# Two-layer hybrid decoder step: the means of squares by a constant 128x128 stationary matrix, the inverse root over 128x264

## The chip, the cores and the metric

The kernel runs on one core of one Trainium2 chip. The metric is device microseconds of one execution; the median of three runs of the kernel before is 2299.41 us (2299.01 to 2299.87). A core has TensorE (PE, matrix products into PSUM), VectorE (DVE), ScalarE (ACT), GpSimd (POOL) and SyncE (SP, here only a queue that issues DMAs). Each engine executes its own queue in program order and waits at semaphores for the others.

## The reference

One inference step over 256 prompt tokens and 8 sample tokens (264 columns), model width 2048, two layers:

```python
def rmsnorm(x, g):
    y = x * lax.rsqrt(jnp.mean(x * x, axis=-1, keepdims=True) + 1e-6)
    return y * g

# one layer
p = rmsnorm(h, norm1_g) @ w_in                  # 2048 -> 10 groups of 512
a, bg, cg, hh, q, k, v, g, u, vv = split(p, 10)
y_a = pool_mixer(a); y_b = conv_mixer(bg, cg, hh)
on  = layernorm_f32(retention(q, k, v))         # over the 128 channels of each of 4 heads
y_c = silu(g) * on * ret_norm_g
y_d = sgu_mixer(u, vv)
h = h + concat(y_a, y_b, y_c, y_d) @ w_out
gt, up = split(rmsnorm(h, norm2_g) @ w_gate_up, 2)
h = h + (silu(gt) * up) @ w_down                # inner width 5632
# after both layers
y = rmsnorm(h, final_norm_g)
```

The mixers' states are outputs too. The change touches the five RMS norms and the two retention layer norms.

## The kernel before, in words

Activations lie transposed: channels on the 128 partitions, the 264 tokens on the free axis, so `h` is 16 tiles of 128x264. Every weight matrix is read once, in sub-blocks of 8 blocks of 128x128 (512 KB each) by SP's queue into seven `raw` buffers. Each sub-block is split into a high part (`whi`, a ScalarE cast, L270) and a remainder (`wlo`, a VectorE subtraction, L271 through the helper of L120); there are four buffers of each, and `do_split` is called at the start of each sub-block so that three further ones are ready or on their way. The activations are split in the same way, and each 128x128x264 block takes three matmuls in a fast f32 form (`work`, L283): low weight by high activation, high by low, high by high. An output chunk (128 channels) of an inner width of 2048 is two sub-blocks, 48 matmuls. Results collect in four PSUM buffers `acc`; four others, `misc`, serve everything else.

`run` (L300) goes over the chunks of a phase: `work`, then `evac` (the chunk is read out of PSUM by VectorE), then `step()`, which advances each background task (a Python generator) by one `yield`. This fixes the queue of every engine: within VectorE's, a chunk's two weight splits, its evacuation, the background work of its step, then the next chunk's splits. The phases of a layer are "in" (40 chunks, in the order V/K/Q x4, VV, U, G, A, then CG/HH/BG x4), "out" (16 chunks), and three times gate/up and down.

The RMS norm is applied late. The phase before adds the squares of `h` (Square on ScalarE, sums on POOL) into partial sums 128x264; the weights are multiplied with the unnormalised activations, and the evacuation multiplies by the token's inverse root `r`. `rms.stats()` is called after 12 of the first chunk's 16 blocks and `rms.bcast()` later in the second chunk (in the first input phase, which works on four chunks at once, behind the second and the third of them). `stats` calls `token_rsqrt` (L157): the partial sums are the stationary operand, 88 tokens at a time, a column of 1/2048 is the moving one, so the sums arrive with tokens on partitions, 88x3 for the RMS norm. VectorE then takes the inverse root of this small tile in eleven operations (`rsqrt`, L137: a shift, a subtraction from a constant, three Newton steps). `token_bcast` (L172) brings it back to 128 partitions of 264 columns with three matmuls against the identity, and ScalarE copies it to SBUF (L205).

The retention norm is the background task `ret_norm` (L545): per step and head a centring product (L551) with its square and copy on ScalarE; then one `token_rsqrt` for all four heads (88x12); then, head by head in four steps, the broadcast, two VectorE multiplies, and a split of the result into the high and low operand of the "out" phase. Other tasks in the same chunks: `sgu` (L571), `pool` (L452), the convolution in the evacuations of HH and BG.

At the end (L733 to L739) the last norm's `r` is used directly from PSUM by VectorE and from SBUF by POOL to scale the 16 tiles of `h`, which nine DMAs write out.

Of the kernel before, what the change touches and what calls it, by code (L numbers as in the profile page):

```python
# [13 lines left out]
AF = mybir.ActivationFunctionType  # L14
ALU = mybir.AluOpType
AX = mybir.AxisListType

P = 128
L = 2
D = 2048  # L20
KD = D // P
NP = 256
NS = 8
T = NP + NS
# [5 lines left out]
EPS = 1e-6  # L30
# [8 lines left out]
TB = 88  # L39
# [12 lines left out]
def hybrid_step(ctx, tc, I, O):  # L52
    nc = tc.nc
    pe, ve, se, po, sy = nc.tensor, nc.vector, nc.scalar, nc.gpsimd, nc.sync
# [4 lines left out]
    def mk(name, shape, dt=F32):  # L59
        return sb.tile(shape, dt, tag=name, name=name)  # L60

    H4 = [mk(f"h{i}", [P, 4, T]) for i in range(4)]
    h = [H4[k // 4][:, k % 4, :] for k in range(KD)]
# [14 lines left out]
    ident, cent = (sq128[:, i, :] for i in range(2))  # L78
    ccol = mk("ccol", [P, 6 + 4 * 16 + KD])
    kdec, rcnt = ccol[:, 0:4], ccol[:, 6:70].rearrange("p (g t) -> p g t", g=4)  # L80
    mean128, mean2048, gfin = ccol[:, 4:5], ccol[:, 5:6], ccol[:, 70:70 + KD]
# [17 lines left out]
    vns = mk("vns", [NS, GW])  # L99
    i8w = mk("i8w", [NS, 4, NS])  # L100
    stat = mk("stat", [P, 12])
    small = mk("small", [P, 3, 12])

    def ta():
        return tfree.popleft()

    def tf(*ts):
        tfree.extend(ts)

    def ma():  # L110
        return misc.popleft()

    def mf(*ts):
        misc.extend(ts)

    def mm(out, lhsT, rhs, start=True, stop=True):
        pe.matmul(out, lhsT, rhs, start=start, stop=stop)  # L117

    def tt(out, a, b, op, eng=None):
        (eng or ve).tensor_tensor(out=out, in0=a, in1=b, op=op)  # L120

    def stt(out, a, s, b, op0, op1):
        ve.scalar_tensor_tensor(out=out, in0=a, scalar=s, in1=b, op0=op0, op1=op1)  # L123

    def ts(out, a, s1, s2, op0, op1, eng=None):
        if s2 is None:
            (eng or ve).tensor_scalar(out=out, in0=a, scalar1=s1, scalar2=None, op0=op0)
        else:
            (eng or ve).tensor_scalar(out=out, in0=a, scalar1=s1, scalar2=s2, op0=op0, op1=op1)
# [4 lines left out]
    def f(ap):  # L134
        return ap.bitcast(F32)

    def rsqrt(out, m, t):  # L137
        ts(t.bitcast(I32), m.bitcast(I32), 1, None, ALU.logical_shift_right, None)
        ts(out.bitcast(I32), t.bitcast(I32), -1.0, float(0x5F3759DF), ALU.mult, ALU.add)
        for _ in range(3):  # L140
            stt(t, out, -0.5, out, ALU.mult, ALU.mult)
            tt(t, t, m, ALU.mult)
            stt(out, t, 1.5, out, ALU.add, ALU.mult)

    def split(src):
        hi, lo = rfree.popleft(), rfree.popleft()
        se.copy(hi[:], src)  # L147
        tt(lo[:], src, f(hi[:]), ALU.subtract)
        return hi, lo
# [4 lines left out]
        stt(lo[:], src, s, f(hi[:]), ALU.mult, ALU.subtract)  # L154
        return hi, lo

    def token_rsqrt(srcs, wcol):  # L157
        n = len(srcs)
        ps = ma()
        for c in range(3):  # L160
            cc = slice(c * TB, (c + 1) * TB)
            for i, parts in enumerate(srcs):
                for x, part in enumerate(parts):
                    mm(ps[:TB, c * n + i:c * n + i + 1], part[:, cc], wcol, x == 0, x == len(parts) - 1)
        w = 3 * n
        m, t, r = (small[:TB, q, :w] for q in range(3))
        ts(m, ps[:TB, :w], EPS, None, ALU.add, None)
        mf(ps)
        rsqrt(r, m, t)
        return r  # L170

    def token_bcast(ps, r, i, n):  # L172
        for c in range(3):
            mm(ps[:, c * TB:(c + 1) * TB], r[:, c * n + i:c * n + i + 1].to_broadcast([TB, P]), ident[:TB, :TB])

    class Rms:
        def __init__(self, second=KD - 1):
            self.parts = []
            self.second = second
            self.n = 0  # L180

        def add(self, src, eng=None):
            s = ta()
            if eng:
                tt(s[:, :T], src, src, ALU.mult, eng)
            else:
                se.activation(s[:, :T], src, AF.Square)  # L187
            if self.n in (0, self.second):
                self.parts.append(s)
            else:  # L190
                a = self.parts[-1]
                tt(a[:, :T], a[:, :T], s[:, :T], ALU.add, po if self.n < self.second else ve)
                tf(s)
            self.n += 1

        def stats(self):
            assert self.n == KD
            self.r = token_rsqrt([[p[:, :T] for p in self.parts]], mean2048)
            tf(*self.parts)

        def bcast(self, both=False):
            ps = ma()
            token_bcast(ps, self.r, 0, 1)
            r = ta()
            se.copy(r[:, :T], ps[:, :T])  # L205
            mf(ps)
            return (r, ps) if both else r

    def to_x(k, gcol):
        scaled(XH[k][:], h[k], gcol)  # L210
        stt(XL[k][:], h[k], gcol, f(XH[k][:]), ALU.mult, ALU.subtract)
# [149 lines left out]
    def in_phase(l, cs, rms, hooks=None):  # L361
        X = {}

        def bcast():
            r = X["r"] = rms.bcast()
            X["rt"] = []
            rt = X["rt"] = [ta() for _ in range(4)]
            for i in (2, 3, 0, 1):
                tt(rt[i][:, :T], tabs[:, i, :], r[:, :T], ALU.mult, po)
            if l == 0:  # L370
                layer_loads(0)
# [179 lines left out]
        def ret_norm():  # L551
            sq, xc = {}, {}
            yield
            for j in range(4):
                yield
                ps = ma()
                mm(ps[:, :T], cent, oT[j][:, :T])
                sq[j], xc[j] = ta(), ta()
                se.activation(sq[j][:, :T], ps[:, :T], AF.Square)
                se.copy(xc[j][:, :T], ps[:, :T])  # L560
                mf(ps)
                tf(oT[j])
            yield
            rn = token_rsqrt([[sq[j][:, :T]] for j in range(4)], mean128)
            tf(*sq.values())
            yield
            for j in range(4):
                yield
                ps = ma()
                token_bcast(ps, rn, j, 4)  # L570
                t = xc[j]  # L571
                tt(t[:, :T], ps[:, :T], t[:, :T], ALU.mult)
                mf(ps)
                stt(t[:, :T], t[:, :T], cols[:, C_RG + j:C_RG + j + 1], gs[j][:, :T], ALU.mult, ALU.mult)
                mix[8 + j] = split(t[:, :T])
                tf(t, gs[j])
# [58 lines left out]
    def gu_phase(cs, rms, r2):  # L635
        act = []
        X = {"r": r2}

        def bcast():
            X["r"] = rms.bcast()  # L640

        def evac(c):
            r = X["r"]
            if not c["up"]:
                t, s = ta(), ta()
                tt(t[:, :T], c["ps"][:, :T], r[:, :T], ALU.mult)
                se.activation(s[:, :T], t[:, :T], AF.Sigmoid)  # L647
                tt(s[:, :T], s[:, :T], t[:, :T], ALU.mult, po)
                tt(s[:, :T], s[:, :T], r[:, :T], ALU.mult, po)
                tf(t)  # L650
                X["s"] = s
            else:
                s = X["s"]
                tt(s[:, :T], c["ps"][:, :T], s[:, :T], ALU.mult)
                act.append(split(s[:, :T]))
                tf(s)

        if rms is None:
            run(cs, list(zip(XH, XL)), evac)
        else:  # L660
            run(cs, list(zip(XH, XL)), evac, rms.stats, bcast)
        return act, X["r"]

    def dn_phase(l, cs, act, last):
        rms = Rms() if last else None

        def evac(c):
            n = c["n"]
            tt(h[n], h[n], c["ps"][:, :T], ALU.add)
            if last:  # L670
                if l + 1 < L:
                    to_x(n, cols[:, C_G1 + n:C_G1 + n + 1])
                rms.add(h[n])
                if l + 1 == L:
                    scaled(h[n], h[n], gfin[:, n:n + 1])

        run(cs, act, evac)
        for pair in act:
            rfree.extend(pair)
        return rms  # L680

    with tc.manual_schedule():
        se.dma_start(out=cols[:], in_=I["cols"][0])
        state["load"] = state["split"] = 1
        src = subs[0]["src"]
        for k in (0, 4):
# [10 lines left out]
        rms = Rms(10)  # L697
# [21 lines left out]
        for kind, l, g, cs in phases:  # L719
            if kind == "in":  # L720
                in_phase(l, cs, rms, hooks if l == 0 else None)
            elif kind == "out":
                rms = out_phase(l, cs)
# [4 lines left out]
            else:  # L728
                last = g == len(FGROUPS) - 1
                rms = dn_phase(l, cs, act, last)  # L730
                if last:
                    tf(r2)
        rms.stats()  # L733
        r, ps = rms.bcast(True)
        for k in range(KD):
            on_pool = k in (4, 8, 12, 15)
            tt(h[k], h[k], (r if on_pool else ps)[:, :T], ALU.mult, po if on_pool else ve)
        for k0, k1 in ((0, 1), (1, 3), (3, 4), (4, 6), (6, 8), (8, 10), (10, 12), (12, 14), (14, 16)):
            sy.dma_start(out=O["y"][:, k0:k1], in_=H4[k0 // 4][:, k0 % 4:k0 % 4 + k1 - k0])  # L739

# [106 lines left out]
```

## Time and profile before

| | us |
|---|---|
| median of three runs | 2299.41 |
| span of the profiled execution | 2298.7 |
| PE busy | 2276.2 |
| DVE busy | 1350.1 |
| ACT busy | 944.1 |
| POOL busy | 289.4 |

The span is the time from the first to the last instruction of the one profiled execution; the page gives no time around it, and 0.71 us is the difference between the median and this span. Busy time counts an engine's instructions without waits. A matmul's record is longer than the slot it takes, since records overlap; slots are read from the chain in order of time, where merged pieces follow one another. "L120" and "L117" are lines of helpers (`tt`, `mm`), so tiles and shapes tell the groups apart. The granted TensorE clock is 0.998 of full over the span.

### The profile page before, as it was taken

What the parts mean: (1) busy time and instruction counts of PE and PEld (TensorE: products, weight loads), DVE (VectorE), ACT (ScalarE), POOL (GpSimd) and SP (SyncE); (2) the same over time, 40 slices, a digit from 0 to 9 for tenths busy, and PEclk for the clock granted to TensorE, in tenths of its full rate; (3) what the DMA queues carried; (4) which work ended last, traced back from release to release, by engine and by line L of the source; (5) the groups of instructions that cost most, each with busy time, mean ns of one, the idle gap of its engine ahead of it and who ended that gap; (6) DMA issues with size and microseconds to landing.
All of it is one profiled execution on the core that took longest, in us unless ns stands there. A gap on an engine that the chain in (4) does not pass through costs nothing.

```text
span 2298.7 us, 44403 instructions
## 1 busy us (share of the span) xinstructions
PE 2276.2 (99%) x18650; PEld 2263.9 (98%) x18650; DVE 1350.1 (59%) x1822; ACT 944.1 (41%) x1267; POOL 289.4 (13%) x404
## 2 busy tenths in 40 slices
PE   8999999999999999999999999999999999999997
PEld 7999999999999999999999999999999999999997
DVE  7558755555455555555665686655554555545554
ACT  5344344444334433343533433544443344333444
POOL 4112111111001110011121211111100111001111
PEclk9999999999999999999999999999999999999999
DMA  8565556656656656565655555556665566665653
GB/s 302 159 190 166 175 179 204 194 181 183 182 171 189 182 167 198 176 182 154 200 176 173 183 169 167 189 175 184 181 185 180 179 183 183 182 179 181 181 152 120
DMA packets 120314, 415.84 MB, mean 181 GB/s; under 512 B 14392, under 2 KB 14808, under 8 KB 120112
## 3 DMA queue, kind: packets, MB, share of 16 engines
q1 hardware_dynamic: 117792, 406.83, 58.1%
q0 software_dynamic: 2176, 6.13, 0.7%
q8 instruction: 146, 2.39, 0.4%
q14 instruction: 56, 0.46, 0.1%
q10 hardware_dynamic: 144, 0.03, 0.0%
HBM read 404.80 MB, written 8.13 MB: 180 GB/s over the span
## 4 chain that ended last, share of the span: by engine, by line
PE 99%; DVE 1%; issue 0%; DMA 0%; ACT 0%; SPq 0%; DVEq 0%; ACTq 0%
PE acc L117 95%; PE ms L117 3%; DMA h<-in_x 0%; DVE h L120 0%; DVE xl L123 0%; DVE wlo L120 0%; PE ms L587 0%; PE ms L490 0%; PE ms L491 0%; DVE small L123 0%; ACT whi L270 0%; ACT vhl L345 0%; ACT xh L132 0%; DVE small L120 0%; ACT t L187 0%
## 5 line engine op out<-in xcount | busy, mean ns | idle before, releaser
L120 DVE TENSOR_TENSOR wlo<-raw,whi 128x1024 fp32r<-128x1024 f32 (+1 forms) x769 | 978.0, 1279 | 658.7 <-ACT whi L270 652.6
L117 PE MATMUL acc<-xh,wlo 128*128 128x264 f32 x4096 | 1172.1, 286 | 8.9 <-DVE wlo L120 7.7
L117 PE MATMUL acc<-xl,whi 128*128 128x264 f32 x4096 | 1164.2, 284 | 0.2
L117 PE MATMUL acc<-xh,whi 128*128 128x264 f32 x4096 | 1162.2, 284 | 0.0
L270 ACT CAST whi<-raw 128x1024 fp32r<-128x1024 f32 (+1 forms) x767 | 781.9, 1029 | 613.8 <-PE acc L117 391.8
L117 PEld LDWEIGHTS acc<-xh,wlo 128*128 128x128 f32 x4096 | 773.8, 189 | 15.1 <-ACT xh L132 6.5
L117 PEld LDWEIGHTS acc<-xl,whi 128*128 128x128 f32 x4096 | 774.0, 189 | 1.9 <-DVE xl L123 1.4
L117 PEld LDWEIGHTS acc<-xh,whi 128*128 128x128 f32 x4096 | 770.4, 188 | 0.0
L117 PE MATMUL acc<-r,whi 128*128 128x264 f32 x3840 | 703.9, 284 | 0.0
L117 PEld LDWEIGHTS acc<-r,whi 128*128 128x128 f32 x3840 | 596.2, 188 | 0.0
L117 PE MATMUL acc<-r,wlo 128*128 128x264 f32 x1920 | 546.9, 285 | 0.0
L120 POOL TENSOR_TENSOR t<-t,t 128x264 f32<-128x264 f32 x281 | 220.4, 784 | 1749.7 <-ACT t L647 1245.2
L117 PEld LDWEIGHTS acc<-r,wlo 128*128 128x128 f32 x1920 | 361.2, 188 | 0.0
L120 DVE TENSOR_TENSOR t<-acc,t 128x264 f32<-128x264 f32 (+2 forms) x288 | 123.8, 430 | 112.4 <-PE acc L117 111.7
L147 ACT CAST r<-t 128x264 fp32r<-128x264 f32 x112 | 46.3, 413 | 292.9 <-DVE t L120 266.9
L647 ACT ACTIVATE t<-t 128x264 f32<-128x264 f32 x88 | 37.4, 425 | 190.8 <-DVE t L120 190.8
L120 DVE TENSOR_TENSOR h<-h,acc 128x264 f32<-128x264 f32 x128 | 54.5, 427 | 51.0 <-PE acc L117 50.7
L120 DVE TENSOR_TENSOR r<-t,r 128x264 fp32r<-128x264 f32 x112 | 48.5, 433 | 53.8 <-ACT r L147 53.8
L132 ACT ACTIVATE xh<-h,cols 128x264 fp32r<-128x264 f32 x64 | 31.7, 513 | 91.9 <-DVE h L120 91.8
L123 DVE SCALAR_TENSOR_TENSOR xl<-h,cols,xh 128x264 fp32r<-128x264 f32 x64 | 35.3, 565 | 28.1 <-ACT xh L132 28.1
L187 ACT ACTIVATE t<-h 128x264 f32<-128x264 f32 x74 | 29.9, 412 | 27.2 <-DVE h L120 27.2
L123 DVE SCALAR_TENSOR_TENSOR sst<-ms,ks,sst 128x128 f32<-128x128 f32 x64 | 18.0, 344 | 13.9 <-PE ms L117 9.2
(103 smaller groups left out, 405.6 us busy)
## 6 DMA issues: line engine op xcount, KB each, us to landing
raw<-in_w_gu SPq DMA_DIRECT2D x352, 512.0 KB, 4.2
raw<-in_w_dn SPq DMA_DIRECT2D x160, 512.0 KB, 3.7
raw<-in_w_in SPq DMA_DIRECT2D x159, 512.0 KB, 4.3
raw<-in_w_out SPq DMA_DIRECT2D x64, 512.0 KB, 4.4
raw<-in_w_dn SPq DMA_DIRECT2D x32, 256.0 KB, 3.5
sst<-in_s_ret SPq DMA_DIRECT2D x16, 256.0 KB, 4.3
out_ret_s<-sst POOLq DMA_DIRECT2D x16, 256.0 KB, 3.0
out_y<-h SPq DMA_DIRECT2D x7, 264.0 KB, 2.6
```

Source lines behind the costliest of these rows:

```text
L117: pe.matmul(out, lhsT, rhs, start=start, stop=stop)
L120: (eng or ve).tensor_tensor(out=out, in0=a, in1=b, op=op)
L123: ve.scalar_tensor_tensor(out=out, in0=a, scalar=s, in1=b, op0=op0, op1=op1)
L132: se.activation(out, a, AF.Identity, scale=s)
L147: se.copy(hi[:], src)
L187: se.activation(s[:, :T], src, AF.Square)
L270: se.copy(hi, src)
L647: se.activation(s[:, :T], t[:, :T], AF.Sigmoid)
```

## The change

The sum over partitions and the broadcast become one matmul: a 128x128 stationary matrix whose entries are all 1/2048 (or 1/128), read from the same column by a broadcast access pattern, times the partial sum 128x264. The result is the mean on every partition. The inverse root is then taken over 128x264: Sqrt on ScalarE (with the epsilon as a bias column), reciprocal and one Newton step on VectorE. `Rms.bcast`, `token_rsqrt`, `token_bcast` and the `small` tile are gone; `r` exists from `stats` on. `ret_norm` has two yields fewer, and each head takes its own root. The `Rms` of the inner phases keeps one partial sum instead of two (the sixteenth square is added by VectorE); the first and the last keep two. A Sqrt on a dummy column stands in front of the last down phase. The final multiplies read `r` from SBUF on both engines.

```diff
+    def rsqrt_cols(ps):
+        m, r, t = ta(), ta(), ta()
+        se.activation(t[:, :T], ps[:, :T], AF.Sqrt, bias=epsc[:, 0:1])
+        ts(m[:, :T], ps[:, :T], EPS, None, ALU.add, None)
+        mf(ps)
+        ve.reciprocal(out=r[:, :T], in_=t[:, :T])
+        stt(t[:, :T], r[:, :T], -0.5, r[:, :T], ALU.mult, ALU.mult)
+        tt(t[:, :T], t[:, :T], m[:, :T], ALU.mult)
+        stt(r[:, :T], t[:, :T], 1.5, r[:, :T], ALU.add, ALU.mult)
+        tf(m, t)
+        return r
+
+    def mean_rsqrt(parts, wcol):
+        ps = ma()
+        for x, part in enumerate(parts):
+            mm(ps[:, :T], wcol.to_broadcast([P, P]), part[:, :T], x == 0, x == len(parts) - 1)
+        return rsqrt_cols(ps)
...
     class Rms:
-        def __init__(self, second=KD - 1):
+        def __init__(self, second=KD):
...
-                tt(a[:, :T], a[:, :T], s[:, :T], ALU.add, po if self.n < self.second else ve)
+                tt(a[:, :T], a[:, :T], s[:, :T], ALU.add, po if self.n < min(self.second, KD - 1) else ve)
...
-            self.r = token_rsqrt([[p[:, :T] for p in self.parts]], mean2048)
+            self.r = mean_rsqrt(self.parts, mean2048)
...
         def bcast():
-            r = X["r"] = rms.bcast()
+            r = X["r"] = rms.r
...
-            yield
-            rn = token_rsqrt([[sq[j][:, :T]] for j in range(4)], mean128)
-            tf(*sq.values())
-            yield
             for j in range(4):
                 yield
-                ps = ma()
-                token_bcast(ps, rn, j, 4)
+                rn = mean_rsqrt([sq[j]], mean128)
+                tf(sq[j])
                 t = xc[j]
-                tt(t[:, :T], ps[:, :T], t[:, :T], ALU.mult)
-                mf(ps)
+                tt(t[:, :T], rn[:, :T], t[:, :T], ALU.mult)
+                tf(rn)
...
-        rms = Rms() if last else None
+        rms = Rms(KD - 1 if l + 1 == L else KD) if last else None
...
+        if l + 1 == L and last:
+            se.activation(epsc[:, 1:2], epsc[:, 0:1], AF.Sqrt)
...
+        po.memset(epsc[:], EPS)
...
-        r, ps = rms.bcast(True)
         for k in range(KD):
-            on_pool = k in (4, 8, 12, 15)
-            tt(h[k], h[k], (r if on_pool else ps)[:, :T], ALU.mult, po if on_pool else ve)
+            tt(h[k], h[k], rms.r[:, :T], ALU.mult, po if k in (4, 8, 12, 15) else ve)
```

## Rows read from the trace of the kernel before

**Rows 1.** The page of the kernel before: busy time, share of the span and instructions of each engine (part 1), and the shares of the chain that ended last by engine (part 4).

```profile
PE 2276.2 (99%) x18650; PEld 2263.9 (98%) x18650; DVE 1350.1 (59%) x1822; ACT 944.1 (41%) x1267; POOL 289.4 (13%) x404
...
PE 99%; DVE 1%; issue 0%; DMA 0%; ACT 0%; SPq 0%; DVEq 0%; ACTq 0%
```

**Rows 2.** Groups of instructions by line and form, for TensorE's matmuls (PE) and for its weight loads (PEld): line, engine, operation, output and inputs, shapes, count, then busy us, mean ns of one, and the idle time before them. A 128x264 f32 product makes two records.

```profile
L117 PE MATMUL acc<-xh,wlo 128*128 128x264 f32 x4096 | 1172.1, 286 | 8.9 <-DVE wlo L120 7.7 <-DVE t L120 1.2
...
L117 PE MATMUL ms<-t,sq 128*128 128x264 f32 x16 | 5.7, 438 | 0.0
...
L117 PEld LDWEIGHTS acc<-xh,whi 128*128 128x128 f32 x4096 | 770.4, 188 | 0.0
...
L117 PEld LDWEIGHTS ms<-sq,small 88*128 88x128 f32 x78 | 9.9, 192 | 2.5 <-DVE small L123 2.5
```

**Rows 3.** The chain that ended last, in order of time: start us, length us, engine, tile, line, number of instructions merged. The first is a step with background products and one more 128x264 product than the second has; the third is the step behind chunk HH0; the last two belong to the first gate/up phase.

```profile
193.09 1.40 PE ms L117 x8
...
200.30 1.84 PE ms L117 x10
...
223.23 2.36 PE ms L117 x26
225.59 11.60 PE acc L117 x96
237.19 0.64 PE ms L117 x6
...
384.96 0.86 PE ms L117 x12
```

**Rows 4.** Busy time of each engine in three stretches of the first layer's input phase: us, then PE, PEld, DVE, ACT, POOL busy (instructions), granted clock, DMA share, GB/s.

```profile
192.00:216.00 24.00, 24.00 (x186) 23.13 (x185) 20.28 (x52) 9.35 (x17) 2.33 (x11) 1.00 0.54 179
216.00:240.00 24.00, 24.00 (x203) 23.78 (x202) 19.99 (x46) 9.16 (x14) 2.54 (x6) 1.00 0.49 153
240.00:257.00 17.00, 17.00 (x145) 17.00 (x143) 12.95 (x22) 6.33 (x9) 0.94 (x2) 1.00 0.50 156
```

**Rows 5.** VectorE's timeline from 192 to 262 us: start us, length us, engine, line, operation, output and inputs, count, and the idle time before it with what ended it.

```profile
205.73 1.38 DVE L120 TENSOR_TENSOR t<-t 128x271 f32<-128x271 f32 x3
...
219.96 0.63 DVE L120 TENSOR_TENSOR t<-t,t 128x264 f32<-128x264 f32 x1
...
225.23 0.42 DVE L120 TENSOR_TENSOR t<-acc,t 128x256 f32<-128x256 f32 x1
...
227.73 0.16 DVE L127 TENSOR_SCALAR small<-ms 88x12 f32<-88x12 f32 x1
...
230.88 2.35 DVE L120 TENSOR_TENSOR wlo<-raw,whi 128x1024 fp32r<-128x1024 f32 x2
233.15 0.42 DVE L120 TENSOR_TENSOR t<-acc,t 128x264 f32<-128x264 f32 x1
234.05 0.43 DVE L120 TENSOR_TENSOR r<-t,r 128x264 fp32r<-128x264 f32 x1 [0.48 <-ACT r L147]
...
246.75 0.81 DVE L123 SCALAR_TENSOR_TENSOR t<-t,cols,t 128x264 f32<-128x264 f32 x1
```

**Rows 6.** The timeline of all engines at the end of the kernel, the multiplies of the final norm and the issue of the output.

```profile
2289.15 4.16 DVE L120 TENSOR_TENSOR h<-h,ms 128x264 f32<-128x264 f32 x12 [1.58 <-ACT t L205]
2289.20 2.85 POOL L120 TENSOR_TENSOR h<-h,t 128x264 f32<-128x264 f32 x4 [8.50 <-ACT t L205]
```

**Rows 7.** VectorE's groups by line and form.

```profile
L123 DVE SCALAR_TENSOR_TENSOR t<-t,t 128x256 f32<-128x256 f32 x8 | 3.4, 425 | 0.5
L120 DVE TENSOR_TENSOR t<-ms,sbrow 128x256 f32<-128x256 f32 x8 | 3.3, 412 | 0.0
...
L120 DVE TENSOR_TENSOR t<-t,t 128x16 f32<-128x16 f32 x8 | 1.4, 175 | 0.3
```

**Rows 8.** ScalarE's timeline in the stretch of rows 5.

```profile
233.61 0.41 ACT L147 CAST r<-t 128x264 fp32r<-128x264 f32 x1 [3.98 <-DVE t L120]
233.93 2.00 ACT L270 CAST whi<-raw 128x1024 fp32r<-128x1024 f32 x2
```

**Rows 9.** The timeline of all engines in the first input phase, 30 to 46 us.

```profile
34.10 0.16 DVE L127 TENSOR_SCALAR small<-ms 88x3 f32<-88x3 f32 x1 [1.46 <-PE ms L117]
...
36.31 1.23 DVE L120 TENSOR_TENSOR wlo<-raw,whi 128x1024 fp32r<-128x1024 f32 x1
...
38.21 3.87 POOL L120 TENSOR_TENSOR t<-tabs,t 128x264 f32<-128x264 f32 x4 [13.58 <-ACT t L205]
...
39.63 1.85 DVE L120 TENSOR_TENSOR wlo<-raw,whi 128x1024 fp32r<-128x1024 f32 x1 [2.09 <-ACT whi L270]
```

**Rows 10.** ScalarE's groups by line and form.

```profile
L132 ACT ACTIVATE r<-ms,cols 128x264 fp32r<-128x264 f32 x8 | 3.9, 493 | 3.6 <-PE ms L117 3.6
...
L709 ACT ACT_TABLE_LOAD x1 | 1.3, 1283 | 1.2 <-PEq L826 1.2
L413 ACT ACT_TABLE_LOAD x1 | 1.3, 1283 | 2.4 <-DVE t L120 2.4
```

**Rows 11.** The chain at the end of the kernel, in order of time: the last sum of squares and the first multiply.

```profile
2284.30 0.96 PE ms L117 x10
2285.28 0.17 DVE small L127
...
2289.15 0.43 DVE h L120
```

More of the change, by code (lines that the diff above doesn't have):

```diff
@@ L101, in hybrid_step @@
     stat = mk("stat", [P, 12])
-    small = mk("small", [P, 3, 12])
+    epsc = mk("epsc", [P, 2])
     def ta():
@@ L155, in split_ps @@
         return hi, lo
-    def token_rsqrt(srcs, wcol):
-        n = len(srcs)
-        ps = ma()
[L160 to L167, printed above, removed]
-        mf(ps)
[L169 to L174, printed above, removed]
     class Rms:
-        def __init__(self, second=KD - 1):
+        def __init__(self, second=KD):
             self.parts = []
@@ L197, in stats @@
             assert self.n == KD
-            self.r = token_rsqrt([[p[:, :T] for p in self.parts]], mean2048)
+            self.r = mean_rsqrt(self.parts, mean2048)
             tf(*self.parts)
[L201 to L207, printed above, removed]
     def to_x(k, gcol):
@@ L562, in ret_norm @@
                 tf(oT[j])
-            yield
-            rn = token_rsqrt([[sq[j][:, :T]] for j in range(4)], mean128)
-            tf(*sq.values())
-            yield
             for j in range(4):
                 yield
-                ps = ma()
-                token_bcast(ps, rn, j, 4)
+                rn = mean_rsqrt([sq[j]], mean128)
+                tf(sq[j])
                 t = xc[j]
-                tt(t[:, :T], ps[:, :T], t[:, :T], ALU.mult)
-                mf(ps)
+                tt(t[:, :T], rn[:, :T], t[:, :T], ALU.mult)
+                tf(rn)
                 stt(t[:, :T], t[:, :T], cols[:, C_RG + j:C_RG + j + 1], gs[j][:, :T], ALU.mult, ALU.mult)
@@ L639, in bcast @@
         def bcast():
-            X["r"] = rms.bcast()
+            X["r"] = rms.r
         def evac(c):
```

## Prediction

> **What bounds the kernel now.** I read the page's busy times and chain first. TensorE is busy 99% of the 2298.7 us span and carries 99% of the chain [rows 1]: the time is the sum of TensorE's slots, plus the few places where it must wait. Next come TensorE's groups with the idle time ahead of them: the main products that use a fresh split (`wlo`) waited 8.9 us in all [rows 2]. So a removed matrix product is worth its slot, and work for another engine costs nothing until it makes a split late. Third, the chain in order of time gives slots: the 12 matmul records of a token-wise sum take 0.86 us, the 6 of a broadcast 0.64, and a 128x264 f32 product 0.44 (10 records 1.84 against 8 records 1.40, which differ by one such product) [rows 3].
>
> VectorE's average of 59% hides the stretch that matters. From 192 to 216 us it is busy 20.3 of 24 us, while TensorE has no gap from 192 to 257 [rows 4], and around the retention norm it runs behind TensorE: the evacuation of chunk HH0, whose product ended at 223.2 [rows 3], begins at 225.23, with the 11 small operations of the inverse root behind it (2.7 us) and only then the two weight splits at 230.88 [rows 5]. VectorE's queue is in program order: a chunk's two splits, the evacuation, the step's background work, the next chunk's two splits.
>
> **Price of one new inverse root on VectorE.** `m` from PSUM 0.37 (twelve independent PSUM products at 0.35 apart [rows 6]); reciprocal R; three dependent operations of Newton at 0.50 (three dependent sums of 271 columns in 1.38 are 0.46 apart [rows 5]; the operations with two reads take 0.425 on 256 columns [rows 7]; 0.04 for the hand-over). No row has a reciprocal. From below I bound R by 0.28 (a 256-column operation at 0.425 less what overlaps), from above by what the same result costs when put together from this engine's own operations, a first guess in two and one Newton step in three, five dependent ones at 0.46 [rows 5]: 2.3 us. I take R = 0.45, the row of one pass, since every f32 operation of 264 columns lies near 0.43; both ends stay in the range. The Trainium skill ("VectorE: DVE Perf Modes", Walkthrough: the 8-slice pipeline in each mode) describes the reciprocal as an iterated divide with a repeat count of 8; no run here shows it yet. A pass costs (412-175)/240 = 1.0 ns an element [rows 7]; if the count means eight passes, that gives an estimate of 0.43+7x0.264 = 2.3 us too, and rival B is the outcome.
>
> **Products on TensorE.** Each of the three inner statistics (both gate/up phases, second input phase) loses 0.86+0.64 and gains one 0.44 [rows 3]: -1.06 each, -3.2 us in all. The first input phase keeps two partial sums, so 0.88 replaces 1.50. A retention norm loses 24 records of sums (2.36-0.44 for the pool product in the same piece = 1.92) and four broadcasts (4x0.64), and gains 4x0.44 [rows 3]: -2.72 per layer. The column broadcast as stationary costs nothing extra: the old broadcast's loads had the same form and the usual slot [rows 2].
>
> **The retention norm on VectorE: the term that decides.** Each head now brings its own root, and the norm starts two chunks earlier (two yields are gone): with HH0, BG0, CG1, HH1 instead of CG1, HH1, BG1, CG2. No DMA is moved with it. Per head, from `m` to the end of the split: 0.37+0.45+3x0.50, then the two multiplies 0.50 and 0.55, ScalarE's cast with its hand-overs 0.49, the subtraction 0.40: 4.3 us. Behind it wait both weight splits, whose ScalarE casts stand in its queue behind that head's cast: 0.55 us until the first is done (1.05 at HH0, where the pool mixer's scaling and subtraction come too), then 2.3 for two splits. Steps on VectorE: HH0 2.50 (225.23 to 227.73 [rows 5]) +4.3+1.05+2.3 = 10.15; BG0 1.3 (product, cast, subtraction [rows 5, 8]) +4.3+0.55+2.3 = 8.45; CG1 0.37+7.15 = 7.5; HH1 2.50+7.15 = 9.65. From 225.2 the steps end at 235.4, 243.8, 251.4 and 261.0, and each step's first split 1.15 earlier: 234.2, 242.7, 250.2, 259.9.
> TensorE needs that first split for the second half of the chunk after next. A chunk is 5.8 us, half of one 2.9 [rows 3]. HH0 ends 223.2; two products 0.88; BG0 until 229.9; 0.44; first half of CG1 until 233.3: it waits 0.9. Second half, 0.44, first half of HH1 until 240.5: waits 2.2. Then BG1's second half is due at 249.0: waits 1.3. CG2's at 256.1: waits 3.8. Together 8.3 us of new waiting, less 2.7 of slots: +5.6 us per layer, **+11.2 for two** (the second layer runs the same code). The same addition for the old order, 225.23+2.50+2.7+0.45+2.3, puts BG0's evacuation at 233.2; its row says 233.15 [rows 5].
>
> **The other statistics.** The old root took eleven small operations, 34.10 to 36.31 [rows 9]; the new one 0.37+0.45+1.5 = 2.3: equal. `Rms` adds one 0.46 add on VectorE behind the last Square, more than 4 us (36 matmuls) before its product: hidden under those; uncovered it would be 0.46 each. Sqrt is a new wait in ScalarE's queue, with the casts of weights behind it; it ends 0.7 us after TensorE reaches the product, well within the 8.7 us by which splits run ahead. In the first input phase the last weight split ends only at 41.48 and holds the evacuation that frees TensorE; a table load 1.28 [rows 10] and Sqrt 0.5 put the root's end at 34.1+1.28+0.5+0.45+1.5 = 37.8; the split then follows at 38.9, the next one, stretched by POOL's products as now (1.85 for 1.23), at about 41.4. TensorE's 0.62 shorter slots are lost in waiting: 0, between -0.6 and +0.6.
>
> **Table loads.** There are two now, 1.283 us each [rows 10]. Sqrt and Sigmoid alternate nine times afterwards, so up to ten if they don't share a table: 8x1.283 = 10.3 us of ScalarE, which is 41% busy [rows 1]. At the retention norm the load ends at 225.3, before VectorE reaches `m` at 227.7; at the gate the splits run three half-chunks (8.7 us) ahead; the last one is put in front of the last phase. Cost 0. The Trainium skill ("ScalarE: Activation LUTs", Table sets: the hidden batching unit) speaks against such alternation and asks 2.7 us a switch; the trace's load is 1.283.
>
> **The tail.** Now 2284.30 (sum) to 2289.15 (first multiply), 4.85 us [rows 11]. Afterwards: product until its result 0.7 (a second record of 0.44, 0.22 after the first [rows 2]), Sqrt 0.5 (a scaled copy out of PSUM [rows 10]), reciprocal 0.45, three at 0.5, hand-overs 0.05: 3.2. The gain is 1.65, but the 12 multiplies then read SBUF beside POOL's four (2.85 us [rows 6]), and beside POOL such an operation took 0.63 and 0.81 instead of 0.43 and 0.49 [rows 5]: two to three of them lose 0.2 to 0.3 each. I take -1.0, between -1.65 and 0.
>
> **Sum** against the profiled execution: +11.2-3.2+0-1.0 = +7.0, span 2305.7. The median of the runs is 0.71 above the span; carried along, **2306.4 us**.
>
> **Rivals.** (B) The reciprocal costs its upper bound, 2.3 us. Each step on VectorE grows by 1.85; the waits become 2.8, 4.1, 3.1 and 5.7 = 15.7 per layer: 2x(15.7-2.7) = +26.0; start +1.85, tail +0.85, slots -3.2: +25.5, 2324.9. For it: nothing in the trace excludes it. Against: it is one instruction, and those are near 0.43.
> (C) The other side: the stock of weight splits covers the norm. Splits run three half-chunks ahead; if background work let the splits pass, or the heads' lag stayed under that stock, no wait arises and the slots alone count: -5.4-3.2-1.0 = -9.6, 2289.8. It decides where a step's VectorE work is under a chunk plus 0.44, 6.25 us. Against: 8 to 10 us by the rows, with a lag of 2 us already there. For: TensorE never waited in this stretch before.
> (D) Half of it: dependent operations come at the 0.35 us of the independent ones [rows 6]; five per head then save 0.75, the waits fall to 0.2+1.5+0.5+3.1 = 5.2, 2x2.5-3.2-1.65 = +0.2: about 2299.6, no change.
> (E) The table loads land on the path after all, at the gate's first Sigmoid and the first root: forecast plus up to 10.3, 2316.7.
>
> **How the numbers follow.** Forecast 0.45 (own range 2300 to 2313), B 0.30, C 0.08, D 0.12, E 0.05. Below 2300 lie C and most of D, above 2326 the upper part of B: the range is 2300 to 2326, forecast 2306.4. About 0.2% (4.6 us) is what a measurement can tell from no change, so 2294.8 to 2304.0 counts as the same: nearly all of D and a sixth of the forecast's chance, 0.18; faster 0.07 (C, less a little); slower 0.75.
>
> **What would show it.** TensorE waits on `wlo` of about 1, 2, 1 and 4 us after HH0's step in both layers, none elsewhere after 60 us; the evacuation of HH1 some 8 us late. `ms` slots of 0.44. The reciprocal's own row decides between the forecast and B. Wrong would be: no `wlo` waits in those steps (C); waits that follow a table load (E).

## The result and the profile after

The changed kernel takes 2324.01 us (median of 4 runs, 2322.83 to 2324.59) against 2299.47 (4 runs): ratio 1.0106, 95% interval 1.0093 to 1.012. It is slower by 24.5 us; the forecast was 2306.4, rival B's time 2324.9.

The page after, parts 1 and 4 (before: [rows 1]):

```profile
PE 2274.4 (98%) x18494; PEld 2258.9 (97%) x18494; DVE 1381.4 (60%) x1806; ACT 957.0 (41%) x1284; POOL 290.5 (13%) x405
...
PE 94%; DVE 4%; issue 1%; ACT 1%; DMA 0%; DVEq 0%; ACTq 0%; SPq 0%
```

TensorE's busy time fell by only 1.8 us, although it has fewer products, because matmuls at half clock (below) count longer; 4% of the chain of waits now lies on VectorE. The groups by line and form (count, then busy us, mean ns of one, idle before) give the new operations and the products that wait (before: [rows 2]):

```profile
L117 PE MATMUL acc<-xh,wlo 128*128 128x264 f32 x4096 | 1177.3, 287 | 30.8 <-DVE wlo L120 27.5 <-DVE t L120 2.9 <-ACT whi L261 0.4
...
L142 DVE RECIPROCAL t<-t 128x264 f32<-128x264 f32 x13 | 23.3, 1793 | 0.0
L117 PE MATMUL ms<-t,ccol 128*128 128x264 f32 x30 | 9.0, 388 | 0.6 <-ACT t L186 0.6
...
L139 ACT ACT_TABLE_LOAD x4 | 5.1, 1283 | 2.8 <-PE ms L117 2.8
```

The wait ahead of the `wlo` products went from 8.9 us to 30.8. The reciprocal, without a row before, takes 1.793 us. TensorE's timeline places the waits (start, length of the matmul, in brackets the wait ahead of it); the first four are layer 0, the last four layer 1:

```profile
235.82 0.39 PE L117 MATMUL acc<-xh,wlo 128*128 128x264 f32 x1 [2.07 <-DVE wlo L120]
245.35 0.39 PE L117 MATMUL acc<-xh,wlo 128*128 128x264 f32 x1 [3.00 <-DVE wlo L120]
253.93 0.39 PE L117 MATMUL acc<-xh,wlo 128*128 128x264 f32 x1 [0.54 <-DVE wlo L120]
264.68 0.59 PE L117 MATMUL acc<-xh,wlo 128*128 128x264 f32 x1 [4.66 <-DVE wlo L120]
...
1378.46 0.39 PE L117 MATMUL acc<-xh,wlo 128*128 128x264 f32 x1 [2.01 <-DVE wlo L120]
1388.00 0.39 PE L117 MATMUL acc<-xh,wlo 128*128 128x264 f32 x1 [1.48 <-DVE wlo L120]
1396.57 0.39 PE L117 MATMUL acc<-xh,wlo 128*128 128x264 f32 x1 [2.04 <-DVE wlo L120]
1407.32 0.59 PE L117 MATMUL acc<-xh,wlo 128*128 128x264 f32 x1 [4.66 <-DVE wlo L120]
```

They are the four places that the prediction named, 10.3 and 10.2 us in all. VectorE's timeline from the evacuation of HH0 on shows what makes them (before: [rows 5]):

```profile
225.71 0.42 DVE L120 TENSOR_TENSOR t<-acc,t 128x256 f32<-128x256 f32 x1
...
228.21 0.43 DVE L127 TENSOR_SCALAR t<-ms 128x264 f32<-128x264 f32 x1
228.55 1.79 DVE L142 RECIPROCAL t<-t 128x264 f32<-128x264 f32 x1
230.38 0.43 DVE L123 SCALAR_TENSOR_TENSOR t<-t 128x264 f32<-128x264 f32 x1
230.84 0.43 DVE L120 TENSOR_TENSOR t<-t,t 128x264 f32<-128x264 f32 x1
231.31 0.43 DVE L123 SCALAR_TENSOR_TENSOR t<-t,t 128x264 f32<-128x264 f32 x1
...
234.54 2.36 DVE L120 TENSOR_TENSOR wlo<-raw,whi 128x1024 fp32r<-128x1024 f32 x2 [0.44 <-ACT whi L261]
```

The two weight splits begin at 234.54, 8.8 us after the evacuation began, and the product that waited for the first of them starts at 235.82. A second effect stands in the granted clock, in the windows of layer 0 (length, busy of PE, PEld, DVE, ACT and POOL, clock, DMA); before, it is 1.00 throughout in the windows of [rows 4]:

```profile
240.00:244.00 4.00, 2.35 (x20) 2.13 (x18) 2.90 (x7) 1.32 (x3) 0.00 (x0) 1.00 0.11 44
244.00:248.00 4.00, 2.65 (x14) 2.65 (x15) 3.93 (x5) 1.36 (x3) 0.80 (x2) 0.74 0.38 110
248.00:252.00 4.00, 4.00 (x28) 3.93 (x28) 3.35 (x7) 0.75 (x2) 0.00 (x0) 0.84 0.44 153
...
260.00:264.00 4.00, 0.01 (x1) 0.00 (x0) 2.87 (x7) 2.00 (x3) 0.00 (x0) 0.87 0.00 0
264.00:268.00 4.00, 3.33 (x15) 3.33 (x16) 3.01 (x5) 2.18 (x4) 0.00 (x0) 0.50 0.51 153
268.00:272.00 4.00, 4.00 (x28) 4.00 (x28) 3.01 (x4) 1.50 (x2) 0.81 (x2) 0.78 0.73 227
```

After the waits of 3.00 and 4.66 us TensorE works for some time at 1.2 instead of 2.4 GHz (clock 0.50). The sum of 4 x (1 - clock) over the four windows with work, less 0.34 for the part of the window from 264 in which it still waited, is 4.2 us; the same sum over layer 1 is 4.6. So layer 0 comes out: 10.3 of waits + 4.2 of clock - the forecast's 2.7 of slots = 11.8; the first gate/up statistic moved from 384.96 [rows 3] to 397.27, that is 12.3 us, of which 0.48 were there already when HH0's product ended.

The tail in the chain of waits, in order of time (start, length; before: [rows 11]):

```profile
2305.41 0.73 PE ms L117 x2
...
2306.16 0.49 ACT t L139
...
2307.11 1.72 DVE t L142
...
2310.25 0.43 DVE h L120
```

and the last group of VectorE's timeline (before: [rows 6]):

```profile
2310.25 6.39 DVE L120 TENSOR_TENSOR h<-h,t 128x264 f32<-128x264 f32 x12
```

From the sum to the first multiply it is 4.84 us, as before (4.85); the twelve multiplies then take 6.39 instead of 4.16.

### The profile page after: what moved, and what is told of

Read it like the earlier page. It is cut to its first block, busy times and chain, and to the rows that moved or that the text cites. A ratio compares the mean times of both kernels' runs of the same rounds, so it can differ in the third digit from the quotient of the medians.

```text
span 2321.5 us, 44097 instructions
## 1 busy us (share of the span) xinstructions
PE 2274.4 (98%) x18494; PEld 2258.9 (97%) x18494; DVE 1381.4 (60%) x1806; ACT 957.0 (41%) x1284; POOL 290.5 (13%) x405
## 4 chain that ended last, share of the span: by engine, by line
PE 94%; DVE 4%; issue 1%; ACT 1%; DMA 0%; DVEq 0%; ACTq 0%; SPq 0%
PE acc L117 91%; PE ms L117 2%; DVE t L123 1%; DVE wlo L120 1%; DVE t L120 1%; DVE t L142 1%; ACT whi L261 0%; DVE t L127 0%; DVE h L120 0%; DVE xl L123 0%; DMA h<-in_x 0%; ACT r L132 0%; PE ms L574 0%; PE ms L482 0%; PE ms L481 0%
## 5 line engine op out<-in xcount | busy, mean ns | idle before, releaser
L117 PE MATMUL acc<-xh,wlo 128*128 128x264 f32 x4096 | 1177.3, 287 | 30.8 <-DVE wlo L120 27.5
```

## The experiments

Theory N: the time lies in the retention norm, on VectorE, and the reciprocal's length decides its size. First, the norm apart from the rest.

**Old retention norm in the changed kernel, and the new one alone in the kernel before.**

The first one's edit to the changed kernel; the second has the reverse of it, in the kernel before:

```diff
+            rn = token_rsqrt([[sq[j][:, :T]] for j in range(4)], mean128)
...
-                rn = mean_rsqrt([sq[j]], mean128)
...
+                token_bcast(ps, rn, j, 4)
```

> The changed kernel with the retention norm of the kernel before (one token-wise root for four heads, 88x12, and its broadcasts); everything else as changed. Theory N (the four roots of the retention norm, each with a reciprocal of 1.79 us, make VectorE late for the weight splits, and the half clock after the longest waits adds to it): the 11.8 and 13.0 us that the two input phases grew by disappear, 2324.0-24.8 = about 2299.2 us, and TensorE waits for no weight split after 60 us. Rival L (the table loads are on the path): the nine loads between Sqrt and Sigmoid are all still there, so at least 2310. Rival T (the end of the kernel and the inner statistics carry the loss): about 2320.

> The kernel before with only the retention norm changed (a root per head over 128x264, two yields fewer); the five RMS norms and the end stay as before. Theory N: the whole loss of the two input phases comes back, 2299.5+24.8 = about 2324.3 us, with waits of about 2, 3, 0.5 and 4.7 us per layer. Rival L: five loads more than before at 1.28, at most 2306. Rival T: about 2300.

Without the new norm: 2300.33 us, ratio 1.0003 (0.9994 to 1.0012), no wait on `wlo` behind 60 us. With it alone: 2323.06, ratio 1.0102 (1.0087 to 1.0117), waits of 2.02, 1.47, 2.05 and 3.11 us in layer 0. Against the 2299.65 of the kernel before, measured beside it, the norm costs 23.4 us of the 24.5, and rivals L and T of these two runs fall. But the first kernel did not gain the 3 us that its shorter slots promise; that is taken up below.

**One pass in place of the reciprocal; no table switch.** The first leaves the inverse out of the result, the second the root.

```diff
-        ve.reciprocal(out=r[:, :T], in_=t[:, :T])
+        ts(r[:, :T], t[:, :T], 0.0, 0.001, ALU.mult, ALU.add)
```
```diff
-        se.activation(t[:, :T], ps[:, :T], AF.Sqrt, bias=epsc[:, 0:1])
+        se.activation(t[:, :T], ps[:, :T], AF.Identity, bias=epsc[:, 0:1])
```

> The changed kernel with each of the 13 reciprocals replaced by a two-operation tensor_scalar of the same 128x264 tile, which leaves the inverse out of the result. Theory N with the reciprocal's length as the mis-sized term: a step loses 1.4 us on VectorE, so the waits fall to the forecast's 1, 2, 1 and 4 us per layer, 2306 to 2309 us (the longest wait may still cost some half clock). Rival C (the count of operations and the two steps' earlier start do it, the reciprocal's length matters little): above 2316.

> The changed kernel with Identity in place of Sqrt, so that ScalarE needs no switch of its table; the root is left out of the result. Theory N: 2324 us, within 1.5, since the loads are hidden except at the first root (1.28 there at most). Rival L: eight loads less, 2314.

With one pass: 2310.11 us, ratio 1.0046 (1.0031 to 1.0061), a little above N's 2306 to 2309. The reciprocals' length alone, in all 13 places, is worth 13.9 us, and with an operation near the length that I had assumed (0.52 by its row, for 0.45) the kernel is still 10.5 us slower. Its waits are 7.2 us in layer 0, where the forecast has 0.9, 2.2, 1.3 and 3.8; the first two in TensorE's timeline:

```profile
233.10 0.39 PE L117 MATMUL acc<-xh,wlo 128*128 128x264 f32 x1 [1.03 <-DVE wlo L120]
241.14 0.39 PE L117 MATMUL acc<-xh,wlo 128*128 128x264 f32 x1 [1.51 <-DVE wlo L120]
```

The other two are 1.03 and 3.67; behind the last one the clock falls here too, 1.7 us in layer 0 by the windows. Without the switch: 2321.39, ratio 1.0094 (1.0077 to 1.0111), 1.1 below N's bounds, with waits like those of the new norm alone (2.13, 1.47, 2.05, 3.13): by the medians the table loads cost some 2.6 us of the 24.5, far from the 10.3 that rival E allows.

**Where the heads stand.** Two runs move the four roots without changing what is executed.

```diff
+            yield
+            yield
             for j in range(4):
                 yield
```
```diff
-                yield
+                for _ in range((2, 3, 3, 2)[j]):
+                    yield
```

> The changed kernel with the two removed yields of the retention norm restored, so that the heads' roots stand in the steps of CG1, HH1, BG1 and CG2 instead of HH0, BG0, CG1 and HH1. Theory N (VectorE's work per head, 4.3 us plus 1.35 for the measured reciprocal, makes the weight splits late wherever the heads stand in consecutive steps): the first head no longer shares HH0's step with the pool mixer; by the same addition as in the prediction, with the reciprocal at 1.76, the waits fall by about 2.4 us a layer, so about 2319. Rival P (the place two chunks earlier is the cause, not the work per head): the old place had no waits, so about 2300.

> The changed kernel with the heads' roots spread: two or three steps lie between a head's root and the next one's, so that VectorE can catch up between them; the same instructions are executed. Theory N: the lag of one head (some 5.5 us of work on VectorE) is worked off in the steps between, so waits of at most 1.5 us remain, 3 us a layer, which the 2.7 us of shorter slots pay for; no half clock after them: 2299 to 2303. Rival P' (one head's chain is already too long for the stock of three half-chunks of splits, wherever it stands): four waits of 2 to 3 us a layer stay, 2312 or more.

At the old place: 2316.86 us, ratio 1.0079 (1.0064 to 1.0095), waits of 4.22, 1.62 and 2.51 in layer 0 (N: about 2319, P: 2300). So the earlier place is not the main cause; it costs 7 us of the 24. Spread: 2305.2, ratio 1.0024 (1.0015 to 1.0033), above N's 2299 to 2303 and far under the rival's 2312. Its waits in layer 0, in TensorE's timeline:

```profile
240.83 0.39 PE L117 MATMUL acc<-xh,wlo 128*128 128x264 f32 x1 [2.11 <-DVE wlo L120]
291.95 0.39 PE L117 MATMUL acc<-r,wlo 128*128 128x264 f32 x1 [1.53 <-DVE wlo L120]
```

So two of four heads wait, and after the first of them the clock falls again, in the windows of this kernel (the clock is the third number from the end):

```profile
240.00:244.00 4.00, 3.17 (x17) 3.17 (x18) 4.00 (x5) 2.36 (x3) 1.67 (x2) 0.71 0.52 138
244.00:248.00 4.00, 4.00 (x31) 4.00 (x30) 3.27 (x8) 1.05 (x1) 0.22 (x2) 0.86 0.93 267
```

N's number was missed by the clock (1.7 us in these two lines, and as much behind the wait of 2.1 us in layer 1) and by the first and last statistics, which this kernel still has in the new form and which are taken one by one next.

**The parts that should gain.** The kernel before with only the three inner statistics new (`True` chooses the new form); then, each put on that kernel alone, the spread norm, the new last norm and the new first statistic.

```diff
-        rms = Rms()
+        rms = Rms(True)
...
-        rms = Rms() if last else None
+        rms = Rms(l + 1 < L) if last else None
```

> The kernel before with only the three inner RMS statistics in the new form (mean product, Sqrt, reciprocal, Newton, one partial sum); first statistic, both retention norms and the last norm as before. By slots, 3 x 1.06 = 3.2 us less, if Sqrt, its table loads and the 1.79 us reciprocal all stay hidden there: 2296.3. Rival (the wide root delays splits there too, some 0.5 to 1 us each, or the table loads land at the gate's first Sigmoid): 2299 to 2301.

> The kernel of the run with only the inner statistics, plus the retention norm in the new form with its heads spread over every second or third step. If the spread heads cost their slots' gain in waits (1.5 us twice a layer): the same as that run, 2296 to 2297. If VectorE catches up fully between heads, the slots alone count, 2.7 us a layer less: about 2291. If single heads still make splits late by 2 us or more: 2302 or more.

> The run with only the inner statistics, plus the last norm in the new form (mean product, Sqrt, reciprocal, Newton, all final multiplies from SBUF, the dummy Sqrt before the last phase). By rows of the changed kernel: the chain from the last sum to the first multiply is 5.83 us against 5.84 before, the twelve VectorE multiplies take 6.39 us against 4.16 and the last store starts about 1.7 us later: 2296.1 + 1.7 = 2297.8. Rival (the tail is covered by the output's DMAs, whose end sets the time): 2296.1, no difference.

> The run with only the inner statistics, plus the first input statistic in the new form. The wait at the first evacuation grows from 1.22 to 2.85 us by the rows of the changed kernel, the slots lose 0.62: +1.0, 2297.1; if the granted clock falls to half after the longer wait, as the matmul at 0.59 us behind it suggests, up to 3.05 us more: 2300.2, with runs spread between the two. Rival (the difference between the run with the old retention norm, 2300.33, and the run with only the inner statistics, 2296.09, comes from the tail alone): 2296.1.

| kernel | median us | ratio to before (95%) |
|---|---|---|
| inner statistics only | 2296.09 | 0.9984 (0.9975 to 0.9993) |
| inner and spread norm | 2300.33 | 1.0004 (0.9995 to 1.0013) |
| inner and new last norm | 2297.39 | 0.999 (0.9981 to 0.9999) |
| inner and new first statistic | 2297.94 | 0.9994 (0.9985 to 1.0003) |

The inner statistics gain 3.6 us (3.2 expected): this kernel is the fastest of all here, faster than the kernel before and the changed one. In its chain of waits a statistic is one piece of 0.45 (before: 0.86 and 0.64 [rows 3]), here that of the second input phase:

```profile
1151.99 0.45 PE ms L118 x2
```

The last norm costs 1.3 us (1.7 expected) and the first statistic 1.85 (1.0 expected, up to 4.1 with a fall of the clock) by the medians; the intervals of both overlap with that of the inner statistics alone. The first statistic's runs spread from 2296.9 to 2300.12. Its trace shows part of the reason, in the chain of waits (start, length):

```profile
33.64 1.08 issue
34.72 0.49 ACT t L140
...
35.66 1.72 DVE t L143
...
41.99 11.87 PE acc L118 x96
```

The 1.08 belong to the table load ahead of Sqrt; then comes the reciprocal. The matmul at 41.99 waited 2.85 us for the evacuation (before 1.22). From the start of the statistic's product to this matmul it is 9.54 us, against 8.66 in the kernel with only the inner statistics: 0.9 more. In the run with the old retention norm the same 96 matmuls behind this wait took 14.59 us instead of 11.87, with the first at 0.59 us, the length it has at half clock. That the spread of the runs comes from this fall is likely: the three longest, 2299.52 to 2300.12, have a granted clock of 0.996, the eight others 0.997. It is not shown, as none of the three has a trace.

The spread norm lost 4.2 us on top, between the named outcomes: about no difference, a gain of 5, or 2302 and more if single heads make splits late by 2 us or more. Its waits are 7.4 us, 3.7 a layer, and 5.4 of slots are saved; that leaves 2.0. The rest is not the clock, which in this trace is 1.00 in all windows around the waits, here those of the first:

```profile
236.00:240.00 4.00, 1.87 (x16) 1.66 (x15) 2.94 (x6) 2.94 (x4) 0.00 (x0) 1.00 0.00 0
240.00:244.00 4.00, 4.00 (x35) 4.00 (x35) 4.00 (x5) 2.32 (x3) 1.71 (x2) 1.00 0.74 225
```

A part of it is that a wait costs more than the idle time in the brackets, which begins only where the overlapping record before it ends. In TensorE's timeline the starts lie 2.41 and 0.23 us apart, where 0.12 is usual, so that the bracket of 2.13 stands for 2.40:

```profile
237.32 0.28 PE L118 MATMUL acc<-xh,whi 128*128 128x264 f32 x1
239.73 0.39 PE L118 MATMUL acc<-xh,wlo 128*128 128x264 f32 x1 [2.13 <-DVE wlo L121]
239.96 0.28 PE L118 MATMUL acc<-xl,whi 128*128 128x264 f32 x1
```

Two further sub-blocks of layer 0 begin some 0.2 late (at 257.78 and 275.82) without a bracket. With 0.27 for each of two waits and 0.4 for these, a layer has 3.7 + 0.9 - 2.7 = 1.9 us more, the two 3.8 of the 4.2. VectorE's timeline at its first head shows where the 2.1 us wait begins:

```profile
230.69 0.43 DVE L121 TENSOR_TENSOR r<-t,r 128x264 fp32r<-128x264 f32 x1 [0.48 <-ACT r L166]
232.48 0.43 DVE L128 TENSOR_SCALAR t<-ms 128x264 f32<-128x264 f32 x1 [1.36 <-ACT t L140]
232.83 1.79 DVE L143 RECIPROCAL t<-t 128x264 f32<-128x264 f32 x1
```

Here the table load is on the path after all: in this step Sqrt stands in ScalarE's queue behind a cast of BG0's evacuation (the convolution's result is split there), which itself waits for VectorE, so load and Sqrt start only then, and VectorE waits 1.36 for them.

**Two attempts at a better spread.** The heads one step later (CG1, CG2, CG3, BG3); then the earlier spread with logarithm and exponential on ScalarE instead of Sqrt and reciprocal.

```diff
-                for _ in range((2, 3, 3, 2)[j]):
+                for _ in range((3, 3, 3, 2)[j]):
```
```diff
-        se.activation(t[:, :T], ps[:, :T], AF.Sqrt, bias=epsc[:, 0:1])
+        se.activation(t[:, :T], ps[:, :T], AF.Ln, bias=epsc[:, 0:1])
+        se.activation(r[:, :T], t[:, :T], AF.Exp, scale=-0.5)
...
-        ve.reciprocal(out=r[:, :T], in_=t[:, :T])
```

> The run with inner statistics and spread heads, with the heads moved by one step each: CG1, CG2, CG3 and BG3 instead of BG0, BG1, BG2 and HH3. In the run before the waits came at the head in BG0 (2.1 us, VectorE still behind from HH0) and in HH3 (1.6 us, where the evacuation alone takes 2.5 us of VectorE), none at BG1 and BG2. If a head fits into a step whose other VectorE work is small and which VectorE enters without lag, only the last one waits, about 1.6 us a layer against 2.72 of shorter slots, and the clock stays up: 2296.1 - 2.2 = 2293.9. Rival (any fourth head costs a wait of 2 us or more, and the one next to the output phase also delays the output products): 2297 or more.

> The run with inner statistics and spread heads (BG0, BG1, BG2, HH3), with Sqrt and reciprocal replaced by ScalarE's logarithm and exponential of minus a half of it; the Newton step stays. VectorE loses 1.79 us per root, ScalarE gains one activation (0.49). If the reciprocal is what still makes the spread heads late (waits of 2.1 and 1.6 us a layer, 1.79 of work more than without it), the waits fall to 0 to 0.5 us a layer and the slots' 2.72 stay: 2296.1 - 5.4 + 0 to 1.0 = 2290.7 to 2291.7. Rival (the chain's length counts, not VectorE's work: the second activation and the table loads take the reciprocal's place): waits as before, 2300.

The first: 2306.69 us, ratio 1.0031 (1.0019 to 1.0043). TensorE's waits behind 60 us, in all, times, longest:

```profile
PE acc L118 <- ACT r L166: 10.0, 2, 5.0
...
PE acc L118 <- DVE wlo L121: 0.9, 2, 0.4
```

The weight splits wait only 0.9 us now, so the reading of the heads in CG steps held; but the fourth head, next to the output phase, delays its own operand by 5.0 us a layer, with a fall of the clock behind it (0.61 in the window from 292 to 296 us): the rival. The second: 2300.32, ratio 1.0004 (0.9995 to 1.0013), no faster than with Sqrt and reciprocal: the rival again. Its waits are 3.7 us in layer 0, as before: the first falls from 2.1 to 1.7 and the last from 1.6 to 0.2, but the heads in BG1 and BG2 now bring one of 0.9 each. VectorE at the first head:

```profile
233.34 0.43 DVE L128 TENSOR_SCALAR t<-ms 128x264 f32<-128x264 f32 x1 [1.36 <-ACT t L140]
235.07 0.43 DVE L124 SCALAR_TENSOR_TENSOR t<-t 128x264 f32<-128x264 f32 x1 [1.30 <-ACT t L141]
```

and ScalarE's groups:

```profile
L140 ACT ACT_TABLE_LOAD x11 | 14.1, 1283 | 0.2
L141 ACT ACT_TABLE_LOAD x11 | 14.1, 1283 | 0.3
```

Each of the 11 logarithms and each of the 11 exponentials brings a load of its own. Load and exponential (1.28 + 0.42) lie where the reciprocal's 1.79 lay, and VectorE waits for them: from `m` to the first operation of Newton it is 1.73 us here, 2.18 with the reciprocal. So what delays the splits is the length of a head's chain, whichever engine it is on, because VectorE's queue stands behind it. The same chain without the loads was not run.

## Why the prediction came out as it did

- **The number: 2324.01 against 2306.4.** It lies outside the forecast's own 2300 to 2313; the stated range of 2300 to 2326 holds it only because rival B was in it.
- **What bounds the kernel; the place and mechanism of the cost: right.** TensorE waits for `wlo` at the four places named, in both layers, and for nothing else of weight behind 60 us.
- **The failed step is the term R: "I take R = 0.45, the row of one pass, since every f32 operation of 264 columns lies near 0.43".** It is 1.79 us, four times that. With a single pass of 0.52 us in its place the kernel ran at 2310.11, which is the forecast plus 3.7; with the reciprocal it ran 13.9 us slower still. The upper bound, 2.3, was the nearer end. The Trainium skill's repeat count of 8 ("VectorE: DVE Perf Modes", Walkthrough: the 8-slice pipeline in each mode) gave 2.3 as an estimate of eight passes; the row is under it, but nearer to it than to one pass.
- **A term that was not in the sum: the clock.** 4.2 us in layer 0 and 4.6 in layer 1 by the windows. It also changes how the waits read: while TensorE runs at half clock it falls behind, and the next wait is shorter (the third wait is 0.54 in layer 0, where the clock fell before it, and 2.04 in layer 1, where it did not). The prediction's own addition with 1.76 for R gives 13.5 us of waits per layer; 10.3 and 10.2 were seen, and with 4.2 of clock layer 0 has 14.5.
- **Rival B came near, 2324.9 against 2324.01, partly by errors that cancel:** its reciprocal is 0.5 us too long, its waits (15.7 a layer against 10.3) too large, its last norm 0.45 too good (+0.85 against +1.3), and it has no clock, which cost 4.2 and 4.6 us. That it met the time so closely is luck.
- **Products: right.** The three inner statistics were -3.2, measured -3.6 in the kernel that has only these; slots of 0.45 for 0.44.
- **First statistic: 0 was forecast,** with ±0.6; the trace has +0.9, with the table load and the reciprocal on its path, and the medians +1.85.
- **Tail: -1.0 was forecast,** between -1.65 and 0; +1.3 was measured. The reciprocal takes back what the shorter chain gave (4.84 against 4.85), and "two to three of them lose 0.2 to 0.3 each" was too few: the mean of all twelve multiplies is 603 ns, 422 before, by VectorE's groups in the changed kernel and then in the kernel before:

```profile
L120 DVE TENSOR_TENSOR h<-h,t 128x264 f32<-128x264 f32 x12 | 6.4, 603 | 0.0
```
```profile
L120 DVE TENSOR_TENSOR h<-h,ms 128x264 f32<-128x264 f32 x12 | 4.2, 422 | 1.6 <-ACT t L205 1.6
```

- **Table loads: the count of ten held,** at 1.283 each, and so did "cost 0" at the retention norm of the changed kernel. It does not hold in the first input phase, nor for a head whose Sqrt stands behind another cast.

The parts measured alone add up: 23.4 - 3.6 + 1.85 + 1.3 = 23.0, against 24.5 for the whole. Of the 1.5 us left over, about 1 lies in layer 0, where waits and clock together are 14.5 us in the whole kernel and 13.6 (8.65 and 4.9) in the one with the new norm alone; why they differ is not shown.

## What to carry to other kernels

Where one engine sets the time and another runs close behind it, price a chain by its latency in the second engine's queue, at the step where it stands, and look at the lag there first: the same four roots cost 23.4 us in four consecutive steps and 4.2 when spread. An instruction that no row shows is the first thing to measure, since "one instruction" is not one pass. And take a change apart: the part with no chain near a busy VectorE, three statistics, was a gain of 3.6 us inside a loss of 24.5.

## What the runs showed of the hardware

- A reciprocal of 128x264 f32 on VectorE takes 1.79 us, its two-operand neighbours 0.43.
- A wait of TensorE costs more than its bracket of idle time: for a bracket of 2.13 us the following products started 2.40 us later than without it.
- After the waits of 3.0 to 5.0 us in these traces TensorE's granted clock stood at half for some microseconds; 4.2 us of work were lost in layer 0 of the changed kernel, 40% on top of its waits. Waits between 2.0 and 2.9 us went either way: 2.11 in the spread kernel was followed by it, 2.13 in the kernel with inner statistics and spread norm was not; 2.85 at the first statistic was in one run's trace and not in another's. Single ones of 1.5 to 1.7 were not (clock 1.00 behind 291.95 in the spread kernel).
- Twelve VectorE multiplies from SBUF beside four on POOL took 6.39 us; with one operand from PSUM, 4.16, beside the same four, which themselves took 3.65 instead of 2.85 [rows 6].
- Logarithm and exponential in turn load a table each time, 1.283 us a load.
